# A two-layer hybrid generator block: sink as a score column, low halves at entry on VectorE, key blocks in the order of their making

## The chip, the core and the metric

The program runs on one core of a Trainium2 chip. Its metric is the device time of one execution in microseconds (us). Before the change the median of three runs is 1187.32 us (1184.21, 1187.32, 1190.15). The rows below come from one more execution, taken by the hardware profiler.

## The reference

512 latent and 256 context tokens of width 1024 go through two layers. Each is an adaLN-modulated RMS norm, a mixer, and a gated residual. Layer 0's mixer is a bidirectional chunkwise mLSTM with four heads; layer 1's is windowed grouped-query attention with 16 heads, four to each key group, where a query block of 128 tokens sees its own block, the neighbours on both sides, and the context. Only the latent stream is returned. The part that the change rewrites is the softmax with a sink, a logit for each head that takes part in maximum and sum and has no value:

```python
def sink_softmax(scores, sink):
    m = sink
    for s in scores:
        m = jnp.maximum(m, jnp.max(s, axis=-1))
    exps = [jnp.exp(s - m[..., None]) for s in scores]
    den = jnp.exp(sink - m)
    for e in exps:
        den = den + jnp.sum(e, axis=-1)
    return tuple(e / den[..., None] for e in exps)

def modulate(a, g, shift, scale):
    return rms_norm(a, g) * (1 + scale) + shift

# layer 1
q = rms_norm(q.reshape(b, t, AT_HEADS, AT_HEAD_DIM), q_g)
p_loc, p_ctx = sink_softmax((s_loc, s_ctx), sink_f[None, None, :, :, None])
```

## The kernel before

Activations lie feature-major: x[j] is a tile of 128 features by 768 tokens (latent columns 0 to 511, called TL wide, then 256 context columns), eight of them. A product of float32 accuracy is made of three passes: each operand is split into a high half (a cast, mostly on ScalarE, L98) and a low half (a subtraction, L104, on VectorE or GpSimd), and PE multiplies high by high, high by low and low by high (`mm3`, L192). Weights come as 512 KB units through `load_w`: DMA into `wraw` (two buffers), cast to `whi`, subtraction to `wlo` (three buffers each); its argument names the engine of the subtraction.

The order on each engine is set by a list scheduler that reads the program; `after(...)` tells it that what follows may not be placed ahead of the named instructions. It adds no semaphore. An accumulator tile in PSUM is guarded as a whole: an engine that reads or writes it waits for the one before.

**Entry.** After the statistics, `rs` (L277) makes 1/rms for the latent columns, L285 scales x[0] by it, and `mod_rows`, `mod_cols` and `mod_quarter` (L234 to L237) give the modulation columns `modc`. `enter` (L292) then makes the first modulated tile: L294 on ScalarE reads `modc`, L297 casts the high half into HL (latent) or HC (context), L298 on VectorE subtracts the low half. The same is done for x[0]'s context columns at L308 to L311. In the same time the first two weight units are loaded (L324), with their low halves on GpSimd (`ge`). PE keeps itself busy with products of zeros (`warm`), then begins the first projection, pqk.

**pv().** In layer 0 each head h projects its values (`v_proj`: six token blocks, in the order 0 to 5, where 4 and 5 are context; the blocks 2i and 2i+1 share a PSUM tile), splits each as it is finished, and `pv` multiplies them by the decayed scores `pl`, four feature blocks e, each over the six key blocks. The value halves of head 0 lie in xb and vgb, of the others in vga and vgb.

**Attention.** 16 steps, group g by query block n. `front(g, n)` works in two half-steps p2, each for two heads, e = 0 and 1: ten matmuls write one score tile `sc` (Lsc, three PSUM banks, one buffer: local scores of e = 0 end at column 512, the context scores of both lie at 512 to 1023, local ones of e = 1 follow), VectorE takes the negative maximum (L1133), multiplies it by 1/rms of the query (`rq`, L1135) and takes the minimum with the negative sink (L1136), and ScalarE makes two exponentials with their sums (L1139). After both half-steps, L1142 to L1145 add exp(sink - maximum) to the sums and invert them, and L1149 (ScalarE) and L1151 (VectorE) scale the probabilities. `back(g, n)` transposes the probabilities (LT, L1165), splits them into PT (L98, L104), multiplies by the values (Lpv, L1169), and L1174 and L1175 gather the result in o. The code runs `front` of a step ahead of `back` of the step before, with pieces of `queries`, `gate_z` and `w_out1` (Lq, Lz, Lwo) beside them by a table PLAN.

## Time and profile before

| | before |
|---|---|
| median of three runs | 1187.32 us |
| profiled execution | 1185.67 us |
| its span, first to last instruction | 1183.6 us |
| mean granted clock of TensorE | 0.994 |
| PE busy | 1147.7 us (97%) |
| PE weight loads | 967.1 us (82%) |
| VectorE busy | 750.5 us (63%) |
| ScalarE busy | 544.2 us (46%) |
| GpSimd busy | 193.3 us (16%) |
| chain that ended last | PE 79%, VectorE 9%, ScalarE 4%, DMA 3% |

2.07 us of the profiled execution lie outside its span. Times of the trace are microseconds from the span's start. Matmul ends are modelled, and a matmul's duration overlaps the next one's; what PE does in a stretch is read from the starts. A bracket behind a row gives the idle time ahead of it on its engine and the instruction that ended it.

### The profile page before, as it was taken

Reading aid. Unit: us, or ns where it says so; the run is one execution under the profiler, and the core shown is the slowest. Engines: PE = TensorE matmul, PEld = TensorE weight load, DVE = VectorE, ACT = ScalarE, POOL = GpSimd, SP = SyncE. Lnnn points to the kernel's source line nnn. Section 1 sums busy time; section 2 is a strip of 40 time slices with the busy share of each in tenths; the row PEclk is TensorE's granted clock in tenths of the full one; section 3 lists DMA queues with packets and bytes.
Section 4 is the critical chain, followed back from the end, with each engine's and each line's share of the span. In section 5 each row is a group of like instructions: output and inputs, shape, how many; then the busy total and the mean of one; then the engine's idle time right before and its main releaser. Section 6 shows DMA issues by size and latency. Waiting matters only on the chain.

```text
span 1183.6 us, 16048 instructions
## 1 busy us (share of the span) xinstructions
PE 1147.7 (97%) x6335; PEld 967.1 (82%) x6335; DVE 750.5 (63%) x1169; ACT 544.2 (46%) x904; POOL 193.3 (16%) x186
## 2 busy tenths in 40 slices
PE   7999999999999999999999999999999898999997
PEld 4778887888878888878888887888998787777876
DVE  5538666275927932681963368274777597969886
ACT  5444423334334232433323333343675477666763
POOL 2010420152212002301200330110221012111100
PEclk9999999999999999999999999999999999999999
DMA  9721321241215412212532112323203641314102
GB/s 346 296 71 24 116 85 54 72 139 56 74 54 195 135 57 71 76 54 75 181 115 72 58 58 71 123 61 124 69 22 98 196 107 36 107 37 128 36 16 71
DMA packets 36011, 113.49 MB, mean 96 GB/s; under 512 B 4945, under 2 KB 7905, under 8 KB 35041
## 3 DMA queue, kind: packets, MB, share of 16 engines
q1 hardware_dynamic: 34848, 106.71, 27.0%
q0 software_dynamic: 1088, 5.77, 2.3%
q8 instruction: 49, 0.80, 0.3%
q14 instruction: 26, 0.20, 0.1%
HBM read 104.98 MB, written 7.48 MB: 95 GB/s over the span
## 4 chain that ended last, share of the span: by engine, by line
PE 79%; DVE 9%; ACT 4%; DMA 3%; issue 2%; POOL 2%; SPq 0%; DVEq 0%; ACTq 0%; POOLq 0%
PE pz L192 11%; PE po L192 11%; PE pqk L192 11%; PE pv L192 10%; PE pwo L192 7%; PE ppv L651 6%; PE psc L192 3%; PE Lq L192 3%; PE Lwo L192 2%; PE Lpv L1169 2%; PE LT L1165 2%; DVE negm L1133 1%; DVE wlo L104 1%; PE Lz L192 1%; DVE PT L104 1%
## 5 line engine op out<-in xcount | busy, mean ns | idle before, releaser
L98 ACT CAST whi<-wraw 128x1024 fp32r<-128x1024 f32 x102 | 106.9, 1051 | 187.6 <-PE pwo L192 51.4
L104 DVE TENSOR_TENSOR wlo<-wraw,whi 128x1024 fp32r<-128x1024 f32 x84 | 104.5, 1245 | 50.0 <-ACT whi L98 49.9
L192 PE MATMUL pz<-HL,whi 128*128 128x512 f32 x256 | 95.3, 396 | 0.0
L192 PE MATMUL po<-HL,whi 128*128 128x512 f32 x256 | 95.2, 396 | 0.0
L192 PE MATMUL pqk<-HL,whi 128*128 128x512 f32 x240 | 89.9, 408 | 3.9 <-ACT HL L297 3.9
L192 PE MATMUL pv<-whi,HL 128*128 128x512 f32 x256 | 83.2, 392 | 0.0
L104 POOL TENSOR_TENSOR wlo<-wraw,whi 128x1024 fp32r<-128x1024 f32 x18 | 44.4, 2473 | 233.6 <-ACT whi L98 224.7
L192 PE MATMUL pz<-HC,whi 128*128 128x256 f32 x256 | 71.6, 280 | 0.0
L192 PE MATMUL po<-HC,whi 128*128 128x256 f32 x256 | 71.5, 279 | 0.0
L192 PEld LDWEIGHTS pqk<-HL,whi 128*128 128x128 f32 x240 | 45.6, 192 | 19.9 <-ACT HL L297 4.3
L192 PEld LDWEIGHTS pz<-HL,whi 128*128 128x128 f32 x256 | 48.1, 188 | 12.4
L192 PEld LDWEIGHTS po<-HL,whi 128*128 128x128 f32 x256 | 48.1, 188 | 12.3
L192 PEld LDWEIGHTS pv<-whi,HL 128*128 128x128 f32 x256 | 48.1, 188 | 11.2 <-DVE vgb L104 1.2
L192 PE MATMUL pqk<-HC,whi 128*128 128x256 f32 x192 | 53.6, 279 | 0.0
L192 PE MATMUL Lq<-HL,whi 128*128 128x512 f32 (+1 forms) x192 | 53.5, 364 | 0.0
L104 DVE TENSOR_TENSOR PT<-LT,PT 128x512 fp32r<-128x512 f32 x72 | 48.2, 684 | 7.9 <-ACT PT L98 7.4
L1169 PE MATMUL Lpv<-PT,V 128*128 128x512 f32 x144 | 51.9, 424 | 1.0 <-DVE PT L104 0.5
L192 PE MATMUL Lwo<-G,whi 128*128 128x512 f32 (+1 forms) x160 | 47.0, 369 | 6.0 <-ACT G L98 2.8
L192 PE MATMUL po<-HL,wlo 128*128 128x512 f32 x128 | 51.6, 403 | 0.4 <-DVE wlo L104 0.4
L192 PE MATMUL pz<-HL,wlo 128*128 128x512 f32 x128 | 51.4, 402 | 0.0
L213 DVE CUSTOM_DVE_ANT_0 junk<-qkp 128x1024 bf16<-128x1024 f32 x40 | 48.8, 1219 | 4.0 <-DMA qkp<-ada 3.6
L98 ACT CAST PT<-LT 128x512 fp32r<-128x512 f32 x72 | 39.2, 589 | 24.9 <-PE LT L1165 22.9
(399 smaller groups left out, 3178.9 us busy)
## 6 DMA issues: line engine op xcount, KB each, us to landing
wraw<-w SPq DMA_DIRECT2D x85, 512.0 KB, 3.5
qkp<-ada SPq DMA_DIRECT2D x30, 512.0 KB, 5.4
wraw<-wo SPq DMA_DIRECT2D x24, 512.0 KB, 3.5
Q<-hl POOLq DMA_DIRECT2D x8, 512.0 KB, 5.9
xa<-xin SPq DMA_DIRECT2D x8, 384.0 KB, 4.7
xb<-xin SPq DMA_DIRECT2D x8, 384.0 KB, 5.1
vga<-ada SPq DMA_DIRECT2D x6, 512.0 KB, 8.8
bc<-negM_d SPq DMA_DIRECT2D x8, 384.0 KB, 3.7
```

Source lines behind the costliest of these rows:

```text
L98: se.copy(dst, src)
L104: return (le or ve).tensor_sub(lo, src, f32(hi))
L192: mm = te.matmul(o, w[s], mv[m], start=first and i == 0, stop=last and i == 2)
L213: ve.tensor_tensor_reduce(out=junk, in0=src, in1=c2[:, v], scale=1.0, scalar=0.0, op0=ALU.mult, op1=ALU.add, accum_out=modc[:, layer, part ...
L651: te.matmul(pb[:, 0:TL], vv[v][:, b, ec], m[:, 0:TL], start=(n == 0 and i == 0), stop=(n == 5 and i == 2))
L1133: ve.tensor_reduce(nmx[:, 0, 2 * p2 : 2 * p2 + 2], both, axis=AX.X, op=ALU.max, negate=True)
L1165: te.transpose(pt[:, i * P : (i + 1) * P], pr[i][:, c : c + P], ident)
L1169: te.matmul(po, V[:, kb, g], hl[:, m], start=(bi == 0 and m == 0), stop=(bi == len(blocks) - 1 and m == 1))
```

## The change

Three edits. At entry the low halves of the first two weight units go from GpSimd to VectorE (the default of `load_w`), and the block that enters the context columns stands behind them in the program. In `pv` the key blocks are taken from 0 to 5. In the attention the sink becomes a column of the score tile: `queries` makes sink times rms for each row (`w`, 20 small VectorE rows in all five places of a query), `front` has ScalarE copy two such columns into the score tile, one at the outer edge of each head's scores, ahead of the matmuls; the maximum and the exponentials with their sums then read one column more, and the minimum with the negative sink and the four steps with `es` are reduced to one reciprocal. The probability rows are two columns wider (642), and those of even heads start at their second column.

```diff
@@ -305,10 +305,6 @@
         enter(j, 1, xr, hf)
 
     hi_0 = enter(0, 0, xr_0, hf_0)
-    with after(xr0, hi_0):
-        rs(TL, T)
-        ve.tensor_mul(xr_0[:, TL:T], x[0][:, TL:T], rstd[:, TL:T])
-        enter(0, 1, xr_0, hf_0)
 
     wgt = t0([P, 3072], F32R, "s")
     acc = [big("pqk") for _ in range(3)]
@@ -321,8 +317,12 @@
                       start=True, stop=False)
     R = ch("R")
     R = [R[:, 0:TL], R[:, TL : 2 * TL]]
-    with after(rstd_exp, copy0):
-        wq = [[load_w(a["w0"][0, u, 0], ge), None] for u in range(2)]
+    with after(rstd_exp, copy0, xr0):
+        wq = [[load_w(a["w0"][0, u, 0]), None] for u in range(2)]
+    with after(xr0, hi_0):
+        rs(TL, T)
+        ve.tensor_mul(xr_0[:, TL:T], x[0][:, TL:T], rstd[:, TL:T])
+        enter(0, 1, xr_0, hf_0)
     st0.append(ada0(1))
 
     def load_raw(src):
@@ -645,12 +645,13 @@
         for e in range(4):
             pb = big("ppv")
             ec = slice(e * P, (e + 1) * P)
-            for n, b in enumerate((4, 5, 0, 1, 2, 3)):
+
+            for n, b in enumerate((0, 1, 2, 3, 4, 5)):
                 hi, lo = pl[b]
                 for i, (v, m) in enumerate(((0, hi), (0, lo), (1, hi))):
                     te.matmul(pb[:, 0:TL], vv[v][:, b, ec], m[:, 0:TL], start=(n == 0 and i == 0), stop=(n == 5 and i == 2))
                     if b >= 4:
-                        te.matmul(pb[:, TL:T], vv[v][:, b, ec], m[:, TL:T], start=(n == 0 and i == 0), stop=(n == 1 and i == 2))
+                        te.matmul(pb[:, TL:T], vv[v][:, b, ec], m[:, TL:T], start=(n == 4 and i == 0), stop=(n == 5 and i == 2))
             se.copy(H[:, e], pb[:, 0:T])
             if e == 0:
                 se.activation(ss, pb[:, 0:T], AF.Square)
@@ -921,8 +922,6 @@
     ve.tensor_scalar(gn[:, 0:2], gn[:, 0:2], 0.125, None, op0=ALU.mult)
     snk = t1([P, 16], F32, "snk")
     sy.dma_start(snk, a["snk"].partition_broadcast(P))
-    nsnk = t1([P, 16], F32, "nsnk")
-    ve.tensor_scalar(nsnk, snk, -1.0, None, op0=ALU.mult)
     bd = t1([P, P], F32, "bd")
     sy.dma_start(bd, a["bd"])
 
@@ -1043,12 +1042,16 @@
             ve.tensor_mul(w, y, y)
             ve.scalar_tensor_tensor(w, w, -0.5, v, ALU.mult, ALU.mult)
             ve.scalar_tensor_tensor(y, w, 1.5, y, ALU.add, ALU.mult)
+
+        ve.tensor_mul(w, v, y)
+        for n in range(4):
+            ve.tensor_mul(w[:, 4 * n : 4 * n + 4], w[:, 4 * n : 4 * n + 4], snk[:, 4 * g : 4 * g + 4])
         rope(qa, qb, ve)
         hl = regroup(qa, qb, TL)
         Q = t1([P, 4, TL], F32R, "Q", 2)
         for m in range(2):
             ge.dma_start(Q[64 * m : 64 * m + 64], hl[m])
-        yield Q, y
+        yield Q, y, w
 
     ones1 = t1([P, P], F32, "ones1")
     ge.memset(ones1, 1.0)
@@ -1077,8 +1080,8 @@
     Qs, szs, Gs, wos = {0: next(q0)}, {}, {}, {}
 
 
-    prow = t_([P, 6, 640], F32, "HC")
-    prow2 = t1([P, 2, 640], F32, "prow2")
+    prow = t_([P, 6, 642], F32, "HC")
+    prow2 = t1([P, 2, 642], F32, "prow2")
     prn = [0]
     szt = t1([P, 4, TC], F32, "szt")
 
@@ -1104,7 +1107,7 @@
 
         return max(n - 1, 0), min(n + 1, 3)
 
-    def front(g, n, Q, rq):
+    def front(g, n, Q, rq, snr):
 
 
         lo_b, hi_b = span(n)
@@ -1113,9 +1116,12 @@
         ts = slice(n * P, (n + 1) * P)
         nmx = t1([P, 2, 4], F32, "negm", 3)
         sums = t1([P, 4], F32, "sums", 3)
-        pr = [prob()[:, 0 : w + TC] for _ in range(4)]
+        rows = [prob()[:, 0 : w + TC + 1] for _ in range(4)]
+        pr = [r[:, 1 - i % 2 : w + TC + 1 - i % 2] for i, r in enumerate(rows)]
         for p2 in range(2):
             sc = mk(ps1, [P, 1536], F32, "sc", 1, "Lsc")
+            i2 = slice(4 * n + 2 * p2, 4 * n + 2 * p2 + 2)
+            se.copy(sc[:, 511 - w : 1025 + w : 513 + 2 * w], snr[:, i2])
             for e in range(2):
                 i = 2 * p2 + e
                 lc = sc[:, 1024 : 1024 + w] if e else sc[:, 512 - w : 512]
@@ -1129,20 +1135,15 @@
                 dst = sc[:, 512 + e * TC : 512 + (e + 1) * TC]
                 te.matmul(dst, Q[:, i, ts], KL[:, g, TL:T], start=True, stop=False)
                 te.matmul(dst, Q[:, i, ts], KH[:, g, TL:T], start=False, stop=True)
-            both = sc[:, 512 - w : 1024 + w].rearrange("p (e c) -> p e c", e=2)
+            both = sc[:, 511 - w : 1025 + w].rearrange("p (e c) -> p e c", e=2)
             ve.tensor_reduce(nmx[:, 0, 2 * p2 : 2 * p2 + 2], both, axis=AX.X, op=ALU.max, negate=True)
-            i2 = slice(2 * p2, 2 * p2 + 2)
-            ve.tensor_mul(nmx[:, 1, i2], nmx[:, 0, i2], rq[:, 4 * n + 2 * p2 : 4 * n + 2 * p2 + 2])
-            ve.tensor_tensor(nmx[:, 1, i2], nmx[:, 1, i2], nsnk[:, 4 * g + 2 * p2 : 4 * g + 2 * p2 + 2], op=ALU.min)
+            ve.tensor_mul(nmx[:, 1, 2 * p2 : 2 * p2 + 2], nmx[:, 0, 2 * p2 : 2 * p2 + 2], rq[:, i2])
             for e in range(2):
                 i = 2 * p2 + e
-                se.activation(pr[i], both[:, e], AF.Exp, bias=nmx[:, 1, i : i + 1], scale=rq[:, 4 * n + i : 4 * n + i + 1],
+                se.activation(rows[i], both[:, e], AF.Exp, bias=nmx[:, 1, i : i + 1], scale=rq[:, 4 * n + i : 4 * n + i + 1],
                               accum_out=sums[:, i : i + 1])
         es = t1([P, 4], F32, "es", 2)
-        ve.tensor_add(es, snk[:, 4 * g : 4 * g + 4], nmx[:, 1])
-        se.activation(es, es, AF.Exp)
-        ve.tensor_add(es, es, sums)
-        ve.reciprocal(es, es)
+        ve.reciprocal(es, sums)
         for i in range(4):
             k = es[:, i : i + 1]
             if i < ACTN:
```

Three places where the order of the built program moves.

VectorE at entry, from the scaling of x[0] by 1/rms (L285) to the second tile (L303). R and modc are the modulation, bc is 1/rms. Before:

```order
L285 TENSOR_TENSOR tmp_201<-xa_76,bc_181 128x512
L278 TENSOR_SCALAR tmp_182<-pstat_115 128x256
L234 TENSOR_TENSOR modc_113<-R_185,adab_72 128x4
L236 TENSOR_TENSOR modc_113<-R_185,bp_114 128x4
L237 TENSOR_TENSOR modc_113<-modc_113,ng_73 128x4
L298 TENSOR_TENSOR HL_213<-rowt_202,HL_213 128x512
L206 TENSOR_TENSOR tmp_184<-tmp_183 128x256
L207 SCALAR_TENSOR_TENSOR tmp_184<-tmp_184,tmp_182 128x256
L208 SCALAR_TENSOR_TENSOR bc_181<-tmp_184,tmp_183 128x256
L310 TENSOR_TENSOR tmp_201<-xa_76,bc_181 128x256
L303 TENSOR_TENSOR tmp_276<-xa_76,bc_181 128x768
L298 TENSOR_TENSOR HC_214<-rowt_202,HC_214 128x256
```

VectorE at the same place, after:

```order
L285 TENSOR_TENSOR tmp_201<-xa_76,bc_181 128x512
L278 TENSOR_SCALAR tmp_182<-pstat_115 128x256
L234 TENSOR_TENSOR modc_113<-R_185,adab_72 128x4
L236 TENSOR_TENSOR modc_113<-R_185,bp_114 128x4
L237 TENSOR_TENSOR modc_113<-modc_113,ng_73 128x4
L104 TENSOR_TENSOR wlo_239<-wraw_236,whi_238 128x1024
L104 TENSOR_TENSOR wlo_245<-wraw_242,whi_244 128x1024
L298 TENSOR_TENSOR HL_213<-rowt_202,HL_213 128x512
L206 TENSOR_TENSOR tmp_184<-tmp_183 128x256
L207 SCALAR_TENSOR_TENSOR tmp_184<-tmp_184,tmp_182 128x256
L208 SCALAR_TENSOR_TENSOR bc_181<-tmp_184,tmp_183 128x256
L324 TENSOR_TENSOR tmp_201<-xa_76,bc_181 128x256
```

The two low halves stand between L237 and the low half of HL; everything else keeps its place.

PE at the first pv of layer 0, behind the last block but one of the value projection (pv_1436 holds value blocks 4 and 5; xb holds high value halves, vgb low ones, qkp the scores). Before:

```order
L651 MATMUL ppv_1606<-qkp_679,xb_1421 128x512 [waits DVE_49,Activation_49]
L653 MATMUL ppv_1606<-qkp_679,xb_1421 128x256
L651 MATMUL ppv_1606<-qkp_679,xb_1421 128x512
L653 MATMUL ppv_1606<-qkp_679,xb_1421 128x256
L651 MATMUL ppv_1633<-qkp_679,xb_1421 128x512 [waits DVE_49]
L192 MATMUL pv_1436<-whi_1517,HC_214 128x512 [waits DVE_49]
L192 MATMUL pv_1436<-wlo_1518,HC_214 128x512
```

PE at the same place, after:

```order
L652 MATMUL ppv_1606<-qkp_679,xb_1421 128x512 [waits DVE_49]
L652 MATMUL ppv_1606<-qkp_679,xb_1421 128x512
L652 MATMUL ppv_1606<-qkp_679,vgb_1420 128x512
L652 MATMUL ppv_1606<-qkp_679,xb_1421 128x512 [waits Activation_49]
L652 MATMUL ppv_1606<-qkp_679,xb_1421 128x512
L652 MATMUL ppv_1606<-qkp_679,vgb_1420 128x512
L652 MATMUL ppv_1606<-qkp_679,xb_1421 128x512
L192 MATMUL pv_1436<-whi_1517,HC_214 128x512 [waits DVE_49]
L192 MATMUL pv_1436<-wlo_1518,HC_214 128x512
```

Seven products of the blocks 0, 1 and 2 stand ahead of the last value block, in place of five of block 4, and the first of them no longer waits for ScalarE.

ScalarE at a step boundary late in the attention (group 3; es and negm are the small tiles of the softmax, prow and HC hold probabilities). Before:

```order
L1139 ACTIVATE prow_7432,sums_9330<-Lsc_9347,negm_9329,nrm_9061 128x640 [waits DVE_49]
L1139 ACTIVATE prow_7432,sums_9330<-Lsc_9347,negm_9329,nrm_9061 128x640
L1143 ACTIVATE es_9363<-es_9363 128x4 [waits DVE_49]
L1174 COPY o_9479<-Lpv_9438 64x256 [waits PE_49,Pool_49]
L98 CAST whi_9824<-wraw_9822 128x1024 [waits DMAHW0_49,PE_49]
L1149 ACTIVATE HC_7431<-HC_7431,es_9363 128x640 [waits DVE_49,Activation_49]
L1149 ACTIVATE HC_7431<-HC_7431,es_9363 128x640 [waits Activation_49]
```

ScalarE at the same boundary, after:

```order
L1143 ACTIVATE prow_7435,sums_9309<-Lsc_9326,negm_9308,nrm_9041 128x641 [waits DVE_49]
L1143 ACTIVATE prow_7435,sums_9309<-Lsc_9326,negm_9308,nrm_9041 128x641
L1175 COPY o_9455<-Lpv_9414 64x256 [waits PE_49,Pool_49]
L1124 COPY Lsc_9465<-nrm_9041 128x2 [waits Activation_49]
L1150 ACTIVATE HC_7434<-HC_7434,es_9342 128x640 [waits DVE_49]
L1150 ACTIVATE HC_7434<-HC_7434,es_9342 128x640
L1175 COPY o_9455<-Lpv_9414 64x256 [waits DVE_49]
```

The exponential of the sink is gone; the copy of the sink columns into the next step's score tile (Lsc_9465) stands behind the first copy of o, which waits for the last value matmul.

## Rows read from the trace of the kernel before

**Rows 1.** The page: busy time of each engine, and the engines of the chain that ended last.

```profile
PE 1147.7 (97%) x6335; PEld 967.1 (82%) x6335; DVE 750.5 (63%) x1169; ACT 544.2 (46%) x904; POOL 193.3 (16%) x186
...
PE 79%; DVE 9%; ACT 4%; DMA 3%; issue 2%; POOL 2%; SPq 0%; DVEq 0%; ACTq 0%; POOLq 0%
```

**Rows 2.** Timeline of VectorE at entry: start us, duration us, engine, line, out<-in.

```profile
21.36 2.78 DVE L285 TENSOR_TENSOR tmp<-xa,bc 128x512 f32<-128x512 f32 x1
...
24.65 1.71 DVE L237 TENSOR_TENSOR modc<-modc,ng 128x4 f32<-128x4 f32 x1
27.89 0.69 DVE L298 TENSOR_TENSOR HL<-rowt,HL 128x512 fp32r<-128x512 f32 x1 [1.53 <-ACT HL L297]
...
31.57 0.43 DVE L298 TENSOR_TENSOR HC<-rowt,HC 128x256 fp32r<-128x256 f32 x1 [0.24 <-ACT HC L297]
```

**Rows 3.** Timeline of GpSimd at entry, the two low halves in one row.

```profile
21.06 5.29 POOL L104 TENSOR_TENSOR wlo<-wraw,whi 128x1024 fp32r<-128x1024 f32 x2 [19.21 <-ACT whi L98]
```

**Rows 4.** Timeline of ScalarE at entry, the first modulated tile.

```profile
26.40 0.81 ACT L294 ACTIVATE rowt<-tmp,modc 128x512 f32<-128x512 f32 x1 [4.46 <-DVE modc L237]
```

**Rows 5.** Timeline of PE at entry, the first projection matmuls.

```profile
27.91 1.52 PE L192 MATMUL pqk<-HL,whi 128*128 128x512 f32 x2 [3.90 <-ACT HL L297]
...
32.95 0.40 PE L192 MATMUL pqk<-HL,wlo 128*128 128x512 f32 x1
33.18 0.40 PE L376 MATMUL pqk<-HC,whi 128*128 128x256 f32 x2
```

**Rows 6.** Windows: length, busy us (instructions) of each engine, granted clock, DMA share, GB/s.

```profile
28.00:30.00 2.00, 2.00 (x4) 1.36 (x5) 1.86 (x4) 0.59 (x2) 0.00 (x0) 0.50 1.04 426
...
900.00:1000.00 100.00, 93.89 (x500) 77.69 (x498) 77.11 (x152) 61.51 (x116) 9.66 (x15) 0.98 0.42 119
1000.00:1100.00 100.00, 94.28 (x515) 77.17 (x515) 87.53 (x176) 67.46 (x135) 15.37 (x23) 1.00 0.29 85
1100.00:1184.00 84.00, 74.66 (x431) 61.18 (x429) 63.28 (x131) 46.15 (x100) 8.79 (x15) 0.97 0.12 38
```

**Rows 7.** Timeline of PE where the first head's pv begins.

```profile
199.80 0.39 PE L192 MATMUL pv<-whi,HC 128*128 128x512 f32 x1
200.86 0.50 PE L651 MATMUL ppv<-qkp,xb 128*128 128x512 f32 x1 [0.68 <-ACT xb L98]
...
201.90 0.39 PE L192 MATMUL pv<-whi,HC 128*128 128x512 f32 x1
```

**Rows 8.** PE's waits over the span: us in total, times, longest us.

```profile
PE Lsc L1122 <- ACT HC L1139: 4.9, 4, 2.1
...
PE Lwo L192 <- ACT G L98: 2.8, 1, 2.8
...
PE ppv L651 <- ACT vga L98: 2.0, 3, 0.7
```

**Rows 9.** The page's groups: low halves on VectorE; busy us, mean ns, idle before.

```profile
L104 DVE TENSOR_TENSOR wlo<-wraw,whi 128x1024 fp32r<-128x1024 f32 x84 | 104.5, 1245 | 50.0 <-ACT whi L98 49.9
```

**Rows 10.** Groups by line and shape in the attention, 933 to 1183.6, VectorE and ScalarE.

```profile
L1136 DVE TENSOR_TENSOR negm<-negm,nsnk 128x2 f32<-128x2 f32 x32 | 4.9, 153 | 0.2
...
L1144 DVE TENSOR_TENSOR es<-es,sums 128x4 f32<-128x4 f32 x16 | 2.9, 183 | 12.1 <-ACT es L1143 12.0
...
L1143 ACT ACTIVATE es<-es 128x4 f32<-128x4 f32 x16 | 3.2, 199 | 0.0
```

**Rows 11.** Timeline of all engines, one turn of the score loop.

```profile
1141.70 0.42 PE L1122 MATMUL Lsc<-KL,Q 128*128 128x384 f32 x1
...
1145.46 0.68 DVE L104 TENSOR_TENSOR PT<-LT,PT 128x512 fp32r<-128x512 f32 x1
...
1146.06 0.15 DVE L1136 TENSOR_TENSOR negm<-negm,nsnk 128x2 f32<-128x2 f32 x1
...
1148.40 0.28 PE L1122 MATMUL Lsc<-KL,Q 128*128 128x256 f32 x1
...
1150.89 0.37 ACT L1174 COPY o<-Lpv 64x256 f32<-64x256 f32 x1 [0.71 <-PE Lpv L1169]
```

## The prediction

> **What bounds the kernel now.** I read the engine summary and the chain that ended last first [rows 1]: PE is busy 97% of the span and holds 79% of the chain, so a part of the change pays only where PE stands still, or where it holds work that others wait for. The second view is the list of PE's waits, the third the timelines around the places that the diff touches. Three stretches matter. At entry PE stands 3.90 us before its first projection matmul [rows 5], and then runs at a granted clock of 0.50, the lower of its two levels [rows 6]. In pv() PE stands 0.68 us before the first matmul of each of the four heads: once behind a cast into xb [rows 7], three times (2.0 us together) behind casts into vga [rows 8]. In the attention PE waits 4.9 us in four waits for the exponentials (L1139) that free the single score tile, and 2.8 us before the last output projection [rows 8].
>
> Durations come from one execution of 1185.67 us, 1183.6 of it span. I forecast the median, so each gain is subtracted from 1187.32; against the profiled execution the same sum is 1.65 lower.
>
> **Entry.** Before, GpSimd makes the two first low halves in 5.29 us from 21.06, until 26.35 [rows 3]. VectorE's L285 runs inside that time: 2.78 us, against 0.69 for the same shape at L298 [rows 2]. L237, four columns, takes 1.71 us and ends at 26.36, in the same hundredth of a microsecond as GpSimd. So VectorE is blocked, and ScalarE's L294 waits 4.46 us for L237 [rows 4]. After, nothing runs on GpSimd there. L285 takes 0.69 and ends at 22.05 in place of 24.14; the three short rows behind it keep their 0.51, so L237 starts at 22.56. At 0.15, the price of a small two-operand row [rows 10], it ends at 22.7. L294 then starts 0.04 later, as before, 3.64 earlier than now; so PE's first matmul comes at about 24.27.
>
> The low halves now stand ahead of L298 on VectorE. At 1.245 each with about 0.08 of overlap [rows 9] they run from 22.7 to about 25.1, and L298, the low half of HL, starts at 25.1 in place of 27.89: 2.79 earlier. That is what is late next: PE's second matmul needs it. L208, L303 and L298 for HC follow it on VectorE and come 2.79 earlier too; HC's low half ends at 29.21 in place of 32.00 [rows 2].
>
> PE: before, twelve matmuls run from 27.91 to 33.18, 0.44 each on average; the last, at full clock, takes 0.23 (32.95 to 33.18) [rows 5]. After, the eleven behind the first start near 25.8, and the gap ahead of them is some 0.3 us and then one of about 1 us in place of 3.90. I take it that the clock then stays up: eleven at 0.23 end at 28.3. The HC matmuls then wait for 29.21, and their twelve take 1.4 us as now: PE is through at about 30.5 in place of 34.6. **Gain 4.1.** If the clock falls all the same, only 2.8 is left, less if the low halves are late: 2.0. Upper end 4.9, the 2.79 and 11 x 0.20 with HC's wait hidden. GpSimd loses 5.29 us of work, and nothing else is queued there in this time.
>
> As for a rule behind these rows: the Trainium skill, in "SBUF — State Buffer", section "Who interferes with whom", says that a VectorE instruction with two SBUF inputs and a GpSimd instruction that reads SBUF take a shared port in turn, each for its whole length. By that alone the return would be what L285 and L237 lose, 3.64 us, and the sum would be 0.5 smaller; the walk through the rows gives more, since PE's clock comes on top, and I keep the walk.
>
> **pv().** The first ppv matmul now uses block 0 in place of block 4. What was late is the high half of the value block of the context (the cast into xb or vga), which v_proj makes second to last, while block 0 is its first. Seven matmuls on the blocks 0 to 2 now run before the last accumulation block of pv. Removed: four waits of 0.68 = 2.7, and around each of them a restart: from 199.80 to 200.86 are 1.06 us where matmuls follow 0.23 apart, so 0.83 are lost, 3.3 in four [rows 7]. The accumulation block behind the seven waits for VectorE's split of block 4: PE comes there 7 x 0.23 = 1.6 after 200.03, in place of 201.90 without a wait [rows 7], so at most 0.25 of new wait can stand there, and I count none. **Gain 3.3**, from 2.0 (some of it met again at blocks 4 and 5) to 4.4.
>
> **Sink column: what goes.** Per half-step (32) the `min` on VectorE, 153 ns; per step (16) two adds, the second of 183, and ScalarE's exponential of 199, for which VectorE waits 12.0 us in all [rows 10]. The `min` costs more than its 153: it stands behind a PT split (1145.46, 0.68) that the scheduler put between it and the product, so it ends at 1146.2, and the exponentials follow [rows 11]. Without it they may start behind the product, 0.68 + 0.15 less the overlap, about 0.7 earlier in a loop of 6.70 us (1141.70 to 1148.40).
>
> **What comes.** 32 copies of 128x2 on ScalarE into the score tile, for which its first matmul waits. The trace has no such copy; its nearest rows are the 199 ns exponential of 128x4 [rows 10] and the 0.37 us copy of 64x256 [rows 11]. I take 0.2, as nearest in size: 6.4 us of ScalarE, between PE's release and PE. At best it lies beside other PE work: cost 0. At worst it is in each loop: 32 x 0.37 = 12. On VectorE 20 small rows of some 0.15 come in `queries`, 3 us; they stand behind the rope's products in its order and none is near a PE wait. Two more columns beside 1280 in a reduce and one beside 640 in an exponential are nothing. Probability rows that start one element later might lose speed on VectorE: none in my sum, at most 16 rows by 0.2 = 3 on an engine that is not the bound.
>
> As the order shows, six or seven copies at step boundaries stand behind `o <- Lpv` (0.37), which waits for the last value matmul of the step before. PE holds that matmul ahead of the scores anyway, and two or three output matmuls between, so I count 0.3 of idle for each, 2.
>
> **Sum for this part.** Only four waits of PE are named for the exponentials; each shrinks by 0.5 (0.7 less the copy): 2.0. Elsewhere PE has other work, but the loop is short of it in the last third: eight loops by 0.25, 2.0. At the end nine Lwo matmuls of 0.119 now stand behind the last Lpv, inside the 2.8 us wait: 1.1. Less 2 for the boundaries: **gain 3.1**. The ends: PE stands 21 us between 900 and 1184 (6.1, 5.7 and 9.3) [rows 6], of which I let at most 9 go; and a loss of 5 where most copies are waited for.
>
> Here a rule speaks against the change. The Trainium skill, in "PSUM — Partial Sum Buffer", section "PSUM bank collisions raise a hardware error", wants two engines kept off one PSUM bank at the same time. The copy lies in the first and third banks of the tile that the matmuls write, so by it no copy can run beside the score matmuls, and all 32 are serial; no run here shows it yet.
>
> **Forecast:** 4.1 + 3.3 + 3.1 = 10.5, so 1187.3 - 10.5 = 1176.8.
>
> **The rivals.** (1) The copies eat the third part and more: each of 32 loops gains 0.7 at 12 places and pays 0.37 at all: 8.4 - 11.8 = -3.4, so 1187.3 - 7.4 + 3.4 = 1183.3. For it: one score tile, ScalarE in order. Against: PE has filler. (2) The clock falls in the new gap at entry as it did in the old: 2.8 in place of 4.1, 1178.1. (3) The entry rows are slow for another cause, such as the loads that fill the DMA engines then, and the change doesn't do what it says there: 0, so 1180.9. (4) The scores of a step no longer start early. Before, the next scores start at 1148.40, while `o <- Lpv` is at 1150.89 [rows 11]; if the copy holds them for it, a boundary costs up to 1150.89 + 0.37 + 0.2 - 1148.40 = 3.1, 15 of them 46. It beats the first two parts from 0.5 a boundary on; at 1.2 it is 18, and the time 1187.3 - 7.4 + 18 = 1198, slower than before. Against it: the new order puts that Lpv ahead of the scores and other matmuls between. (5) The loop is the bound in more places than the waits name, and the removal gives 9: 1170.9.
>
> **How the numbers follow.** Chances: the forecast 0.52, rival 1 0.16, rival 2 0.10, rival 3 0.05, rival 4 0.06, rival 5 0.11. The forecast's own range is 1173 to 1181. The range of 8 in 10 reaches from 1169.5 (half of rival 5 left out) to 1184 (rival 4 and the worse half of rival 1 left out). A measurement of this kernel tells about 0.5%, 5.9 us, from no change: faster means under 1181.4. Nearly all of the forecast, rivals 2 and 5 and half of 3 lie there, and a fifth of rival 1: 0.77. Slower than 1193.3 is rival 4: 0.05. The rest, 0.18, is within.
>
> **What would show it.** In the entry's timeline L285 at 0.69, L237 at 0.15, no POOL row, and a granted clock of 1.00 from 24 to 33: right; a clock of 0.50 is rival 2, an L285 over 2 us rival 3. In pv() the waits of ppv for casts gone, and no new one of over 0.3 us at blocks 4 and 5. In the attention the waits of the scores for the exponentials down from 4.9; if in their place a wait for the copy, or for `o`, of more than 5 us stands in PE's list, rival 1 or 4 is right. The forecast is wrong if the last stretch, from the first scores to the end, is not shorter than before.

## The result and the profile after

The changed kernel takes 1168.15 us (median of four runs, 1165.81 to 1169.61), the kernel before 1187.42 (four runs): a ratio of 0.9843 with a 95% interval from 0.9824 to 0.9862, so 1.6% faster. A second series gives 1167.14 against 1186.56, 0.9836 (0.9815 to 0.9856). The forecast was 1176.8 with a range down to 1169.5: the direction holds, the size does not: the time lies 8.65 below the forecast and 1.35 below the lower end of the range. The profiled execution after is 1169.61 us with a span of 1167.1, where before it was 1185.67 and 1183.6. One execution among those of the experiments, 3445.30 us for the kernel with pv alone where its five others took 1177 to 1183, was a slow one and is left out of every median.

The page of the changed kernel, as in [rows 1]:

```profile
PE 1143.7 (98%) x6335; PEld 968.1 (83%) x6335; DVE 743.0 (64%) x1126; ACT 544.6 (47%) x920; POOL 190.1 (16%) x184
...
PE 81%; DVE 8%; ACT 3%; DMA 3%; issue 2%; POOL 2%; SPq 0%; DVEq 0%; ACTq 0%; POOLq 0%
```

PE is busy 4.0 us less and the span is 16.5 shorter, so 12.5 of the gain is time in which PE stood idle before. Where it was is read from places that both traces have; this table takes the start of each from the timelines of PE.

| place | before | after | shift |
|---|---|---|---|
| first row of R behind the first tile | 34.70 | 30.27 | -4.43 |
| first ppv, head 0 | 200.86 | 195.68 | -5.18 |
| first ppv, head 1 | 335.03 | 328.05 | -6.98 |
| first ppv, head 2 | 537.06 | 528.98 | -8.08 |
| first ppv, head 3 | 739.10 | 729.91 | -9.19 |
| last output projection of layer 0 | 867.14 | 857.67 | -9.47 |
| first scores | 933.77 | 924.22 | -9.55 |
| last Lpv | 1168.00 | 1151.21 | -16.79 |
| last Lwo | 1179.27 | 1162.75 | -16.52 |

So the entry gave 4.4 (0.1 of it an earlier start), pv 5.0, the attention 7.0.

**Entry.** Timeline of VectorE after, against [rows 2]; GpSimd has no row between 20 and 30, where [rows 3] stood:

```profile
21.23 0.69 DVE L285 TENSOR_TENSOR tmp<-xa,bc 128x512 f32<-128x512 f32 x1
...
22.43 0.16 DVE L237 TENSOR_TENSOR modc<-modc,ng 128x4 f32<-128x4 f32 x1
22.50 2.36 DVE L104 TENSOR_TENSOR wlo<-wraw,whi 128x1024 fp32r<-128x1024 f32 x2
24.78 0.68 DVE L298 TENSOR_TENSOR HL<-rowt,HL 128x512 fp32r<-128x512 f32 x1
...
28.29 0.42 DVE L298 TENSOR_TENSOR HC<-rowt,HC 128x256 fp32r<-128x256 f32 x1 [0.24 <-ACT HC L297]
```

L285 is back at 0.69 from 2.78, L237 at 0.16 from 1.71. The timeline of PE, against [rows 5]:

```profile
24.14 0.50 PE L192 MATMUL pqk<-HL,whi 128*128 128x512 f32 x1 [0.29 <-ACT HL L297]
25.52 0.50 PE L192 MATMUL pqk<-HL,whi 128*128 128x512 f32 x1 [0.88 <-DVE HL L298]
...
28.31 0.84 PE L376 MATMUL pqk<-HC,whi 128*128 128x256 f32 x2
...
30.27 1.06 PE L221 MATMUL R<-vgb,ccol 128*32 128x512 f32 x8
```

The windows of the same stretch, against the 0.50 of [rows 6] (columns as there, the granted clock third from the end):

```profile
26.00:28.00 2.00, 2.00 (x11) 1.55 (x9) 1.93 (x4) 0.75 (x2) 0.00 (x0) 1.00 1.02 406
28.00:30.00 2.00, 1.92 (x13) 1.42 (x12) 0.47 (x2) 2.00 (x5) 0.00 (x0) 1.00 1.03 416
```

The wait of 3.90 has become one of 0.29 and one of 0.88 for the low half of HL, and the clock stays at its upper level. It did so in four of the five profiles with this entry. In the fifth, that of the last experiment, L285 starts at 24.00, the two waits are 0.69 and 0.87, and the clock falls behind them:

```profile
30.00:32.00 2.00, 2.00 (x6) 1.63 (x5) 1.25 (x2) 1.97 (x4) 0.00 (x0) 0.50 1.01 416
```

There R comes 10.01 behind L285 in place of 9.04: rival 2 of the prediction in one execution of five.

**pv.** The timeline of PE at the first head, against [rows 7]:

```profile
195.45 0.39 PE L192 MATMUL pv<-whi,HC 128*128 128x512 f32 x1
195.68 0.63 PE L652 MATMUL ppv<-qkp,xb 128*128 128x512 f32 x2
...
197.31 0.43 PE L192 MATMUL pv<-whi,HC 128*128 128x512 f32 x1
```

0.23 between the first two in place of 1.06, and no bracket: nothing is waited for, at 197.31 either.

**Attention.** PE's waits after, against [rows 8] (us in total, times, longest):

```profile
PE Lwo L192 <- ACT G L98: 2.4, 1, 2.4
PE Lsc L1128 <- DMA Q<-hl: 2.2, 1, 2.2
PE LT L1166 <- ACT HC L1150: 2.1, 1, 2.1
...
PE Lsc L1128 <- ACT Lsc L1124: 0.2, 1, 0.2
```

The 4.9 us of waits for the exponentials are gone, and the ppv waits with them. One wait is new, 2.1 ahead of a transpose (LT) for scaled probabilities (L1150). The copy of the sink columns (L1124) is named with 0.2. That looks as if the copies cost nothing; the experiments show otherwise.

### The profile page after: what moved, and what is told of

It reads as the page before. It is cut to its first block, busy times and chain, and to the rows that moved or that the text cites. A ratio compares the mean times of both kernels' runs of the same rounds, so it can differ in the third digit from the quotient of the medians.

```text
span 1167.1 us, 16017 instructions
## 1 busy us (share of the span) xinstructions
PE 1143.7 (98%) x6335; PEld 968.1 (83%) x6335; DVE 743.0 (64%) x1126; ACT 544.6 (47%) x920; POOL 190.1 (16%) x184
## 4 chain that ended last, share of the span: by engine, by line
PE 81%; DVE 8%; ACT 3%; DMA 3%; issue 2%; POOL 2%; SPq 0%; DVEq 0%; ACTq 0%; POOLq 0%
PE pz L192 11%; PE po L192 11%; PE pv L192 11%; PE pqk L192 10%; PE pwo L192 8%; PE ppv L652 6%; PE Lwo L192 4%; PE psc L192 3%; PE Lpv L1170 3%; PE Lq L192 3%; PE LT L1166 2%; PE Lz L192 2%; DVE negm L1139 1%; POOL tmp L584 1%; DVE wlo L104 1%
## 5 line engine op out<-in xcount | busy, mean ns | idle before, releaser
L104 DVE TENSOR_TENSOR wlo<-wraw,whi 128x1024 fp32r<-128x1024 f32 x86 | 107.2, 1250 | 51.5 <-ACT whi L98 49.8
L104 POOL TENSOR_TENSOR wlo<-wraw,whi 128x1024 fp32r<-128x1024 f32 x16 | 39.1, 2447 | 234.0 <-ACT whi L98 225.1
L192 PEld LDWEIGHTS po<-HL,whi 128*128 128x128 f32 x256 | 48.1, 188 | 12.5
L192 PEld LDWEIGHTS pqk<-HL,whi 128*128 128x128 f32 x240 | 44.5, 188 | 16.4 <-issue 2.5
```

Source lines behind the costliest of these rows:

```text
L104: return (le or ve).tensor_sub(lo, src, f32(hi))
L192: mm = te.matmul(o, w[s], mv[m], start=first and i == 0, stop=last and i == 2)
```

## The experiments

All compare with the kernel before on the same chip; the parts, the removals and the rest are three series on three chips. For the attention one reading is used throughout: the turn of the score loop, taken from the timelines. For each of the 32 half-steps it has four parts: from PE's first score matmul to the reduce on VectorE, from there to the first exponential on ScalarE, the exponentials (1.6 in every kernel, not in the table), and from the start of the last exponential (plus 0.77) to the next score matmul. The means, with the whole turn (first to last half-step, divided by 31):

| kernel | to the reduce | reduce to exponential | to the next scores | turn |
|---|---|---|---|---|
| before | 1.97 | 2.96 | 0.58 | 7.14 |
| changed kernel, first profile | 1.85 | 2.16 | 1.30 | 6.92 |
| sink column alone | 1.82 | 2.15 | 1.29 | 6.87 |
| no sink at all | 2.01 | 2.39 | 0.60 | 6.67 |
| no minimum | 2.01 | 2.37 | 0.69 | 6.71 |
| no es steps | 1.85 | 2.98 | 0.62 | 7.09 |
| product and minimum in one | 2.14 | 2.55 | 0.59 | 6.93 |
| minimum twice | 1.97 | 3.64 | 0.45 | 7.68 |
| changed kernel, copies on VectorE | 1.86 | 2.23 | 1.15 | 6.89 |

Three more profiles have the attention of the kernel before (entry alone, pv alone, more warming); their turns are 7.13, 7.07 and 7.12. So a difference of 0.07 a turn, 2 us in 31, can come without a cause in the program.

**The three parts, and the whole again.** The edits are the diff of the change, cut into its pieces: the first two pieces, the piece in `pv`, the rest.

> The whole change again, beside its three parts on the same chip. The trace of the changed kernel puts 4.4 us of its gain at entry, 5.0 in layer 0's pv and 7.0 behind the first scores, together 16.4 of the 16.5 by which its span is shorter; the medians were 19.3 apart. Theory S (the parts are separate and add up): this run is about 16 to 19 us faster than the kernel before, and equals the sum of the next three within 2 us. Rival R (the scheduler's new order as a whole gave it): the parts do not add up; the sum misses this run by 4 us or more.

> The entry alone: the two low halves on VectorE and the context block behind them; pv and sink as before. Theory S: 4.4 us faster, all of it before the first tile is through (first row of R behind L376 4.4 earlier), and nothing gained or lost later than that by more than 1 us. Rival R: the total differs from 4.4 by 3 us or more, because the order of later stretches moves too.

> The order of the key blocks alone. The prediction said 3.3 us; the trace of the whole change shows 5.0 over the four heads (0.83 ahead of each first ppv matmul, 0.2 inside each pv, and 0.8 between the first and the second head). Theory S: 4.5 to 5 us faster, the 0.8 between the heads among it. Rival (0.8 belonged to the entry or to chance of the order): 3.9 to 4.2 faster, with the stretch between the first two heads as before.

> The sink column alone. The prediction said 3.1 us with a range from -5 to 9. Theory S: 7 us faster, all of it behind the first scores; PE's 4.9 us of waits for the exponentials gone. Rival R (the order that the scheduler happened to find with all three parts gave the 7): another amount, under 4 or over 10, with waits for the exponentials left.

| kernel | median us | ratio (95%) | gain us |
|---|---|---|---|
| whole change | 1167.14 | 0.9836 (0.9815 to 0.9856) | 19.4 |
| entry alone | 1181.73 | 0.9954 (0.9940 to 0.9969) | 4.8 |
| pv alone | 1179.97 | 0.9942 (0.9924 to 0.9960) | 6.6 |
| sink column alone | 1176.09 | 0.9917 (0.9899 to 0.9935) | 10.5 |

The parts sum to 21.9, the whole is 19.4: 2.5 apart, half a microsecond more than the 2 that theory S allowed, and less than the 4 of rival R; the medians have spreads of 3 to 6 us, so the parts add up as far as this can be seen. The 10.5 of the sink column lies above the 7 that was expected and just above the 10 from which rival R was to count; but the waits for the exponentials that R wanted left are gone. The traces agree. With the entry alone, R comes 9.04 us behind the start of L285, as in the whole change, against 13.34 before (12.79 to 13.62 in the eight profiles with that entry and the same warming, so the 4.3 is 3.8 to 4.6), and nothing moves from there to the end of layer 0 (-3.37 at 34, -3.30 at 867). With pv alone, 5.5 us are gained between R and the end of layer 0: 1.16, 1.64, 0.93 and 0.92 ahead of the four heads, 0.15 to 0.20 inside each pv, 0.09 behind. The 1.64 is there in every profile: from the end of head 0's pv to head 1's are 113.1 in the nine with the old order and 111.5 in the five with the new. The 1.16 is not: from R to head 0's pv the nine spread from 165.8 to 166.4, the five from 165.0 to 165.4. With the sink column alone, layer 0 gains nothing and the turn is 0.26 shorter, 8.1 in 31. Of this, 1.5 is the first turn (7.15 before, 5.68 here), where the granted clock is 1.00 and was 0.54; in the first profile of the changed kernel, where it is 0.58, the 31 turns are 6.6 shorter.

**The entry, taken apart.** A kernel before with more warming matmuls:

```diff
-WARM, WARM2 = 36, 10
+WARM, WARM2 = 36, 26
```

> The kernel before with 26 warming matmuls in place of 10 ahead of the first projection, so that PE runs through the 3.9 us in which it waits for the first tile; GpSimd and VectorE as before. It splits the entry's gain into clock and earlier data. Theory (both count, as the prediction's walk): the clock stays at 1.00, eleven matmuls run 0.23 apart, the context tiles' low half at 32.00 is then the last wait: PE is through at about 33.4 in place of 34.6, 1.2 of the 4.4. Rival (clock is all): 3 or more. Rival (clock costs nothing, the data alone set the end): 0 within 0.4.

Its time is 1184.40 against 1186.02, 0.9984 (0.9970 to 0.9998). The timeline of PE:

```profile
28.37 0.50 PE L192 MATMUL pqk<-HL,whi 128*128 128x512 f32 x1 [0.36 <-ACT HL L297]
...
32.05 0.84 PE L376 MATMUL pqk<-HC,whi 128*128 128x256 f32 x2
...
34.01 1.06 PE L221 MATMUL R<-vgb,ccol 128*32 128x512 f32 x8
```

From the first matmul to R are 5.64 us, against 6.79 before (27.91 to 34.70): 1.15 for the clock alone (1.00 in each window from 26 to 34), as the walk had it, and 1.6 in the medians. (The same stretch takes 6.24 to 7.08 in the eight profiles with the entry and the warming of the kernel before, so 0.6 to 1.4.) The first matmul comes 0.46 later in this run than in the kernel before, as L285 does (0.41), which does not enter the difference. So of the 4.3 some 1 is the clock, the rest the earlier data.

**What the removals give without the copies.** The kernel before without the sink (its term is missing from the sum, and from the maximum); without the minimum alone; and without the es steps alone (again the term is missing):

```diff
-            ve.tensor_tensor(nmx[:, 1, i2], nmx[:, 1, i2], nsnk[:, 4 * g + 2 * p2 : 4 * g + 2 * p2 + 2], op=ALU.min)
...
-        ve.tensor_add(es, snk[:, 4 * g : 4 * g + 4], nmx[:, 1])
-        se.activation(es, es, AF.Exp)
-        ve.tensor_add(es, es, sums)
-        ve.reciprocal(es, es)
+        ve.reciprocal(es, sums)
```

> The kernel before without the sink in layer 1: no minimum, no es add, exponential and add, no copy into the score tile; the probabilities are divided by the sum without the sink's term. This is the upper bound of what the removals can give, and the copies cost what the sink run (7 us behind the first scores, with the clock at first scores and last projection set aside) is short of it. Theory P (as the prediction priced it: the shorter loop gives 5 or so, the copies take 2 of it back): 9 us faster, so the copies cost 2. Rival F (the copies are free, and the whole 7 is the removals): 7 faster, within 1 of the sink run. Rival R (order by chance): a figure that has nothing to do with either, under 4 or over 11.

> The kernel before with the minimum against the negative sink left out alone; the maximum is that of the scores, the es steps stay as they are. If the exponentials started late because the minimum stood behind a PT split on VectorE, this gives most: 32 loops by up to 0.7, of which PE sees what its waits for exponentials name, 4.9 (theory M: 4 to 6 us faster). Rival E (the es chain at the step's end is what held the loop): under 2.

> The kernel before with the minimum kept and the es chain (add, exponential, add) left out: the division is by the sum without the sink's term. Rival E: 5 or more faster. Theory M: 1 to 3 faster, from the scaling of the probabilities (L1149, L1151), the transposes and the values behind it starting 0.5 earlier in 16 steps. Additive with the run without the minimum to the run without the sink within 1.5, or else the order by chance is of that size.

| kernel | median us | ratio (95%) | gain us |
|---|---|---|---|
| no sink | 1171.15 | 0.9875 (0.9860 to 0.9890) | 14.9 |
| no minimum | 1173.24 | 0.9899 (0.9877 to 0.9922) | 12.8 |
| no es steps | 1182.39 | 0.9976 (0.9963 to 0.9988) | 3.6 |

All three expectations were too small; the 14.9 also lies above the 11 from which the order by chance was to count, so the sizes alone do not exclude it. The 12.8 and the 3.6 make 16.4, 1.5 more than the 14.9, at the edge of what was allowed for parts that add up. One VectorE instruction of 153 ns, 32 times, 4.9 us of an engine that is not the bound, gave 12.8 us when it went: more than the whole sink column (10.5), though the intervals of the two overlap. The copies, with the 20 new rows in `queries`, therefore cost 14.9 - 10.5 = 4.4, a difference of two series that is uncertain by some 3. The timeline of the kernel without the minimum shows the reason:

```profile
1130.42 1.49 DVE L1133 TENSOR_REDUCE negm<-Lsc 128x2 f32<-128x1280 f32 x1
...
1131.94 0.69 DVE L104 TENSOR_TENSOR PT<-LT,PT 128x512 fp32r<-128x512 f32 x1
1132.55 0.15 DVE L1135 TENSOR_TENSOR negm<-negm,nrm 128x2 f32<-128x2 f32 x1
1132.62 0.68 DVE L104 TENSOR_TENSOR PT<-LT,PT 128x512 fp32r<-128x512 f32 x1
1132.73 0.89 ACT L1138 ACTIVATE HC<-Lsc,negm,nrm 128x640 f32<-128x640 f32 x1 [0.23 <-DVE negm L1135]
```

The exponentials start right behind the product, while the second PT split runs; in [rows 11] they came behind that split and the minimum. The turn is 0.43 shorter, 13.3 in 31, and that is the whole gain. Only 6.3 of it is PE standing less in these turns (4.9 in place of 11.2); the other 7.0 is matmul work that now lies behind the start of the last half-step, 163 matmuls there in place of 140, where PE stands 4.7 in place of 7.0. So the loop holds the kernel in more turns than the four that PE's waits name. In how many is not shown: 23 of the 31 turns are shorter and 8 longer, by up to 2.4, as the scheduler places other work.

**Dose.** The minimum once more (it changes nothing in the result), and product and minimum in one instruction for each head:

```diff
             ve.tensor_tensor(nmx[:, 1, i2], nmx[:, 1, i2], nsnk[:, 4 * g + 2 * p2 : 4 * g + 2 * p2 + 2], op=ALU.min)
+            ve.tensor_tensor(nmx[:, 1, i2], nmx[:, 1, i2], nsnk[:, 4 * g + 2 * p2 : 4 * g + 2 * p2 + 2], op=ALU.min)
```

```diff
-            ve.tensor_mul(nmx[:, 1, i2], nmx[:, 0, i2], rq[:, 4 * n + 2 * p2 : 4 * n + 2 * p2 + 2])
-            ve.tensor_tensor(nmx[:, 1, i2], nmx[:, 1, i2], nsnk[:, 4 * g + 2 * p2 : 4 * g + 2 * p2 + 2], op=ALU.min)
+            for e in range(2):
+                i = 2 * p2 + e
+                ve.tensor_scalar(nmx[:, 1, i : i + 1], nmx[:, 0, i : i + 1], rq[:, 4 * n + i : 4 * n + i + 1],
+                                 nsnk[:, 4 * g + i : 4 * g + i + 1], op0=ALU.mult, op1=ALU.min)
```

> The kernel before with the minimum taken twice (the second changes nothing): one more dependent place in each of the 32 half-steps. Theory D: slower by about what the removal gave, 6 to 13 us. Rival T: slower by 0 to 2 (32 x 0.15 is 4.9 of VectorE's time, some of it hidden). Rival R: no relation to dose, faster too.

> The kernel before with product and minimum in one instruction for each head (two of 128x1, which don't wait for one another, in place of a product of 128x2 and a minimum that waits for it): as many VectorE instructions as before, the same result, but no second dependent place behind a PT split. Theory D (the dependent place costs, not the 153 ns): most of the 12.8 us that the run without the minimum gained, 8 to 12 faster. Rival T (VectorE's time in the loop costs): 0 to 2. Rival R (chance of the order): anything, also slower.

Twice: 1202.42 us, 1.0128 (1.0097 to 1.0159), 16.2 slower, above what was expected. One half-step of it:

```profile
1154.36 0.15 DVE L1135 TENSOR_TENSOR negm<-negm,nrm 128x2 f32<-128x2 f32 x1
1154.43 0.68 DVE L104 TENSOR_TENSOR PT<-LT,PT 128x512 fp32r<-128x512 f32 x1
1155.03 0.15 DVE L1136 TENSOR_TENSOR negm<-negm,nsnk 128x2 f32<-128x2 f32 x1
1155.09 0.68 DVE L104 TENSOR_TENSOR PT<-LT,PT 128x512 fp32r<-128x512 f32 x1
1155.69 0.15 DVE L1137 TENSOR_TENSOR negm<-negm,nsnk 128x2 f32<-128x2 f32 x1
1155.88 0.89 ACT L1140 ACTIVATE HC<-Lsc,negm,nrm 128x640 f32<-128x640 f32 x1 [1.19 <-DVE negm L1137]
```

Each small row that depends on the one before lets the scheduler put a split of 0.68 between them. From reduce to exponential are 3.64 in the mean, 0.68 more, and the turn is 0.55 longer, 17.0 in 31. Removed, kept and doubled, the step moves the time by -12.8, 0 and +16.2: the direction follows the dose. That the two sizes are so near is luck. From the first scores to the end PE stands 8.0 us more than before (26.2 in place of 18.3), and it is busy 9.4 us more with the same matmuls, for in four places of the loop, each behind gaps, the clock fell to its lower level, 0.50, and the mean of the window is 0.83; before, it was 1.00 in each window of 10 us from 940 to 1160.

```profile
960.00:970.00 10.00, 9.27 (x45) 7.77 (x46) 8.99 (x23) 7.12 (x15) 3.22 (x5) 0.83 0.90 237
1000.00:1010.00 10.00, 7.05 (x34) 6.06 (x33) 9.11 (x18) 7.85 (x16) 1.94 (x3) 0.83 0.16 52
1090.00:1100.00 10.00, 9.78 (x44) 7.80 (x44) 8.20 (x19) 4.48 (x9) 0.00 (x0) 0.83 0.41 116
1130.00:1140.00 10.00, 8.83 (x39) 7.18 (x40) 6.88 (x14) 4.22 (x10) 1.53 (x1) 0.83 0.09 37
```

In one instruction: 1183.11, 0.9970 (0.9954 to 0.9986), 3.2 faster, where 8 to 12 were expected: a miss. The dependent place is gone and the exponential comes 0.41 earlier, but the two instructions take 265 ns each, 14.7 us in 64, against 9.8 for the 64 they replace, and the scores take 0.17 longer to the reduce. The longer way is one half-step in the main: the scheduler put its tenth score matmul behind Lq matmuls, 6.99 after the first, and the turn is 4.5 longer than before. In the trace the 31 turns are 6.5 shorter, in the medians the kernel is 3.2 faster. So it is not shown that the dependent place is the whole of the 12.8, and the order that the scheduler finds can move a single turn by more than this experiment gained.

```profile
1054.70 0.33 PE L1122 MATMUL Lsc<-KL,Q 128*128 128x384 f32 x1
...
1061.69 0.28 PE L1131 MATMUL Lsc<-KH,Q 128*128 128x256 f32 x1
```

```profile
L1137 DVE TENSOR_SCALAR negm<-negm,nrm,nsnk 128x1 f32<-128x1 f32 x64 | 14.7, 265 | 0.3
```

**The copies.** In the kernel with the sink column alone (groups by line, then the timeline of ScalarE at one step boundary):

```profile
L1123 ACT COPY Lsc<-nrm 128x2 f32<-128x2 f32 x32 | 5.4, 167 | 4.7 <-DVE nrm L1047 4.5
```

```profile
1041.64 0.21 ACT L1142 ACTIVATION_READ_ACCUMULATOR prow<-Lsc,negm,nrm 128x1 f32 x1
1041.74 0.59 ACT L98 CAST PT<-LT 128x512 fp32r<-128x512 f32 x1
1042.20 1.36 ACT L1149 ACTIVATE HC<-HC,es 128x512 f32<-128x512 f32 x2
1043.44 0.60 ACT L98 CAST PT<-LT 128x512 fp32r<-128x512 f32 x1
1043.90 0.20 ACT L1123 COPY Lsc<-nrm 128x2 f32<-128x2 f32 x1
```

The copy takes 0.167, but here 2.05 us of other ScalarE work stand between the exponentials that free the tile and the copy that opens it again. At nine of the 15 step boundaries a copy of `o` stands between, and the sink copy comes 0.1 to 0.8 behind the exponentials; at four others, of which this is one, casts and the scaling of the probabilities (L1149) hold it 1.6 to 2.5. Over all turns that distance is 0.6 in the mean, and from exponentials to scores the table has 1.29 against 0.58: 0.71 a turn, 22 us, which the shorter way from reduce to exponential (0.81) and to the reduce (0.15) pay for.

The copies on VectorE in the changed kernel:

```diff
-            se.copy(sc[:, 511 - w : 1025 + w : 513 + 2 * w], snr[:, i2])
+            ve.tensor_copy(sc[:, 511 - w : 1025 + w : 513 + 2 * w], snr[:, i2])
```

> The changed kernel with the sink copies on VectorE in place of ScalarE. If the copies cost because ScalarE's queue holds them behind o <- Lpv and PT casts (theory Q), VectorE, which is the busier engine but reads the scores itself, changes where they wait: 1 to 3 us either way. If they cost by their own 0.2 ahead of each turn of the loop (theory L), nothing changes within 1.5: the time stays at the changed kernel's.

1167.13, 0.9831 (0.9804 to 0.9857), the changed kernel's time within 0.1, with 1.15 in place of 1.29 from exponentials to scores and 0.07 more from reduce to exponential. By the letter that is theory L (nothing changes within 1.5), but it doesn't tell the two apart: VectorE's queue holds the copy 0.53 in the mean, ScalarE's 0.60, and PE's list now has the copy with 2.0 us in five waits, in place of 0.2 in one.

**A faster kernel.** The changed kernel's entry and pv, with the sink of the kernel before but no minimum (the maximum is that of the scores; exp(sink - maximum) is still added):

> The changed kernel's entry and pv with the kernel before's sink, but without the minimum: the maximum is that of the scores alone, and the es steps still add exp(sink - maximum), which is the same softmax as long as that exponential does not overflow. No copy into the score tile, no new rows in queries. If the parts add up: 4.8 + 6.2 + 12.8 = 23.8 faster than before, 1162 to 1165, and 2 to 4 below the changed kernel. Rival (the parts don't add once the attention is shorter): equal to the changed kernel within 1.5.

1162.81 us, 0.9795 (0.9769 to 0.9821): 23.5 faster than before, where the parts sum to 24.2 (4.8, 6.6 and 12.8), and 4.3 under the changed kernel's median of the second series as under the kernel with copies on VectorE, which ran on the same chip. Its softmax is the same so long as exp(sink - maximum) stays finite. Where a sink could exceed all scores of a row so far that it does not, that would have to be looked after; this was not tried.

## Why the prediction missed

**Entry: right.** The steps came as walked: L285 at 0.69, L237 at 0.16, the first matmul 3.64 us earlier against L285's start (2.91 in place of 6.55), the low half of HL as the next thing waited for, the clock at 1.00, then HC's low half. From L285 to R it is 4.30 where 4.1 was predicted. (The upper end of 4.9 should read 5.0, 2.79 and 11 x 0.20; nothing rests on it.) The clock stayed up in four profiles of five, so rival 2 was a fair one. The 3.64 that the Trainium skill's page "SBUF — State Buffer", section "Who interferes with whom", would give back by itself are just what the first matmul gained; the other 0.66 and the way they come about are PE's.

**pv: right in mechanism, a third too small.** The four waits are gone and nothing took their place. 3.3 was predicted, 5.0 to 5.5 are there. The term that was mis-sized is the count: I took four gaps of 0.83 and left out the 0.15 to 0.20 that PE gains inside each pv (0.7 in all), and the 0.8 more ahead of head 1. (The 0.3 more ahead of head 0 lies within the spread of the profiles.) Most of the 0.8 is no wait: in the projections ahead of head 1, from 222 to 264 before and 220 to 261 with pv alone, 238 matmuls take 41.88 us in the one and 41.27 in the other without a wait, at a granted clock of 1.00 in both. The cause is open.

**Sink column: the step that failed** is the sum, "only four waits of PE are named for the exponentials ... eight loops by 0.25". It took PE's list of waits for a list of the turns in which the loop is the bound. In the other turns PE was never shown waiting for the exponentials, because the scheduler had filled the time with work of Lq, Lz and Lwo, of which there is a fixed amount, and the gaps showed elsewhere, as rows with no or other brackets. PE stood 10.0 us between 940 and 1150 before, and 3.0 between the same times after (before, then after):

```profile
940.00:1150.00 210.00, 200.00 (x1101) 163.12 (x1099) 176.38 (x360) 143.61 (x292) 29.66 (x45) 1.00 0.24 68
940.00:1150.00 210.00, 207.00 (x1158) 171.10 (x1157) 181.07 (x335) 149.29 (x318) 33.74 (x48) 1.00 0.23 68
```

The loop of 7.14 us ran 32 times one behind the other, and its 31 turns became 6.6 us shorter (8.1 with the sink column alone, 1.5 of it the clock in the first turn), where the sum had 4.0 for the turns less 2 for the boundaries. The price per turn, 0.7 less the copy, was right for the first half (0.81) and wrong for the second (0.71 for a copy taken at 0.2): the copy was priced by its duration, not by its place in ScalarE's queue.

The Lwo matmuls behind the last Lpv (nine in the prediction, eleven in the trace) took 0.4 off the final wait (2.8 to 2.4), not 1.1. The six or seven boundaries were priced at 2; there are nine, and they are in the 0.71.

**The rivals.** 1 (copies eat the gain) is half true: 4.4 us. 4 (scores held for `o`) is there at nine step boundaries, but the copy stands 0.1 to 0.8 behind the exponentials there, with the copy of `o` between, rather than 3. 5 (the loop is the bound in more places than the waits name) is what happened, at too small a chance; its 9 for this part lies between the 7.0 of the trace and the 10.5 of the medians. The rule of the Trainium skill's page "PSUM — Partial Sum Buffer", section "PSUM bank collisions raise a hardware error", is kept in the trace: none of the 32 copies lies beside a score matmul, and the scores follow 0.05 us behind the copy at the soonest. By the rule alone a copy could run beside the context scores, which fill the middle bank; that none does follows from the tile being guarded as a whole. What it costs is the place in the queue, on which the rule says nothing.

**Trace against median.** The spans differ by 16.5, the medians by 19.3. The difference is not in the order of the work: the same program's second profile has a span of 1163.6, and the last section says where most of the 3.5 us between the two lies.

## What to carry to other kernels

Where one buffer is filled, read and freed in a loop, write down its turn, part by part, and multiply by the number of turns; a list of the waits of a well-filled engine names only the turns in which the filler ran out. In such a turn a small dependent instruction is priced by what the scheduler puts ahead of it, and a new producer by what stands ahead of it in its queue: here 0.6 to 0.7 us for 0.15. And before a step is moved into another engine's work, see whether it can be left out: the minimum was not needed for the maximum's purpose.

## What the runs showed of the hardware

The granted clock behind PE's two other long waits, at the first scores and before the last projection, differs from one execution of the same program to the next. Windows of the first profile of the changed kernel, then of its second:

```profile
924.20:926.40 2.20, 2.18 (x11) 2.20 (x12) 0.00 (x0) 0.00 (x0) 0.00 (x0) 0.58 0.87 266
1155.30:1159.50 4.20, 4.17 (x23) 4.04 (x24) 1.22 (x3) 0.00 (x0) 0.00 (x0) 0.66 0.17 56
```

```profile
923.70:925.80 2.10, 2.04 (x14) 1.94 (x15) 0.57 (x1) 0.00 (x0) 0.00 (x0) 1.00 0.84 213
1153.20:1157.20 4.00, 3.92 (x31) 3.79 (x32) 1.82 (x5) 0.00 (x0) 0.00 (x0) 1.00 0.20 67
```

The wait ahead of the last projection is 2.41 us in both, yet the clock fell in one and not in the other; ahead of the first scores it is 2.2 and 1.8. With the sink column alone the wait ahead of the first scores is 2.22, as in the first profile, and the clock is 1.00. The fall costs 1.5 us at the end (11.54 against 10.05 from the last Lpv to the last Lwo) and 1.5 at the scores (7.15 against 5.69 for the first turn): 3.0 of the 3.5 us between the two spans. The four runs of the changed kernel in the second series stand in the order of their mean clock, 1164.84 and 1165.66 at 0.998, 1168.62 at 0.996, 1170.68 at 0.994. In the kernel before both places ran at 0.54 and 0.61 in its one profile, and all its runs beside those four have a mean clock of 0.989 to 0.995. A change that shortens such a wait from 2.8 to 2.4 seems to be paid a second time in some runs; how often, these runs are too few to tell.

The other spread is at the start: over the 14 profiles L285 starts between 21.04 and 24.00. In the latest, the loads ahead of it are waited for longer (ScalarE 1.43 for x, PE 2.20 for the modulation's weights) than in the earliest (0.15 and 1.15). So gains at entry are read from a row to a row, not from the span's start.
